# Three transformer blocks in one program: the triangular inverses of block 3 as paced steps over 128 partitions, the relative-bias rows written during block 2

## The chip, the cores and the metric

The program runs on one core of a Trainium2 chip. The metric is device time in microseconds (us) of one execution. A core has a matrix engine (TensorE, PE in the rows below, its weight loads PEld), a vector engine (VectorE, DVE), a scalar engine (ScalarE, ACT), GpSimd (POOL) and a queue engine (SyncE, SP) that issues nearly all transfers between DRAM and the core's memory. ACT can issue transfers too.

## The reference, cut to what matters

One sequence of 512 tokens with 2048 features goes through three blocks. The change concerns two pieces of block 3.

The first is the gated delta rule, in chunks of tokens. With `L` strictly lower triangular, every head and chunk needs the inverse of `I + L`:

```python
L = jnp.where(strict, jnp.einsum("bnhid,bnhjd->bnhij", k_beta, k) * decay, 0.0)
t_inv = lax.linalg.triangular_solve(eye + L, eye, left_side=True, lower=True, unit_diagonal=True)
u = jnp.einsum("bnhij,bnhje->bnhie", t_inv, v_beta)
w = jnp.einsum("bnhij,bnhjd->bnhid", t_inv, k_beta * jnp.exp(g)[..., None])
```

The second is the sliding-window attention, whose logits get a bias that depends on the distance of query and key alone:

```python
bias = rel_bias[t5_bucket(jnp.maximum(dist, 0))]          # dist = query position - key position
logits = jnp.where(valid, logits + bias, -jnp.inf)
```

Around both stand projections by large weight matrices; block 2 (spatial gating and neighbourhood attention) comes between block 1 and block 3.

## The kernel before

Activations are feature-major tiles of 128 x 512. A "unit" is one projection of 128 output columns: 16 steps over the input features, each of three products (`hi*hi`, `hi*lo`, `lo*hi`), summed in a PSUM tile `pm`. Weights come on SP's queue as 128 x 1024 chunks `wr` (three buffers). ACT copies each half of a chunk into `wh`, DVE subtracts it and leaves the rest in `wl` (five buffers each); 12 products use one half. PE's order is fixed in the program, so a late `wl` holds up PE and all that stands behind it.

`drive` runs units one after the other and, between groups of 12 products, advances up to five generators (heads of the delta rule, attention pairs). A bare `yield` of a generator means "go on 12 products later". The build then merges these streams into one fixed order per engine; each engine goes through its rows in order.

**Inverses.** `gdn` makes four generators `inverse(g)`, each for two heads. `inverse_blocks` takes the 32 x 32 diagonal blocks of both heads (32 blocks), writes them to DRAM (`du`) and reads them back with one block per partition (`fs`, 32 partitions). Then 31 steps of substitution run on DVE, step `i` being a product of `i*i` elements into `fp` and a sum into row `i` of `ft`. The result goes back over DRAM (`dt`) into the heads' tiles `acc...`/`km`. All 31 steps are issued in one go, then 16 bare yields pass before the heads may use the result. `inverse_join` (run by `scan`) transposes on DVE and joins the blocks on PE.

**Relative bias.** `rel_bias` makes 16 rows of 384 values (one small product on PE, one sum on DVE) and writes 128 copies of each to DRAM (`reld`, 3 MB) on SP's queue. The attention pairs of block 3 read it back (`t<-reld`). `block3` calls it ahead of `small_products`, which loads `w3s` in six chunks through the same `wr` buffers and the same queue.

`mods` is background work: 1024-column tiles `gr` of two more weight matrices, loaded on SP's queue and summed on DVE during blocks 1 and 2. Its tags `gr` and `ga` are those of `fs`, `fp` and `ft`.

Of the kernel before, what the change touches and what calls it, by code (L numbers as in the profile page):

```python
# [18 lines left out]
P = 128  # L19
# [9 lines left out]
INV_STEPS = 16  # L29
# [10 lines left out]
class Kernel:  # L40
# [44 lines left out]
    def t(self, tag="w", dt=F32):  # L85
        """A [128, 512] tile; each tag hands out its slots in order, so streams that overlap have their own."""
        self.n += 1
        return self.tp.tile([P, T], dt, name=f"t{self.n}", tag=tag, bufs=SLOTS[tag])
# [40 lines left out]
    def tr4(self, src):  # L129
        """128x128 transposes of the four column blocks of src into one bank."""  # L130
# [5 lines left out]
    def rsqrt_cols(self, out, ss, scale, eps):  # L136
        """out = (ss * scale + eps) ** -0.5 on [128, n] with n small."""
# [5 lines left out]
    def bcast_cols(self, cols):  # L143
        """[128, 4] token columns -> [128, 512] rows, the same on every partition (in PSUM)."""
# [23 lines left out]
    def unit_steps(self, w, ct, rhs):  # L168
        """z^T of 128 columns: w is [ct, half, 128, 1024]; rhs the (hi, lo) tiles of each k. Pauses every 12 products."""
# [16 lines left out]
    def first_units(self, w, cts, make):  # L186
        """The first units of a block, k by k, while make(k) gives the (hi, lo) tiles of their operand."""
# [28 lines left out]
    def drive(self, todo, width, fillers=(), done=None):  # L216
        """Runs generators beside the stream of units. A generator yields either a unit that it needs, whose PSUM it
        is sent, or None: products that wait for other engines then come a few products of the stream later.
        Generators start in the order of todo, up to width at a time; fillers keep the stream going beyond that.
        done holds the units that are there already."""  # L220
# [58 lines left out]
    def silu2(self, z, rows=None):  # L279
        """2 * silu of a unit's PSUM (times rows)."""  # L280
# [9 lines left out]
    def block1(self):  # L290
# [5 lines left out]
        # the operand is gain * x; the rms factor of a token is put on every unit as it leaves its PSUM  # L296
# [27 lines left out]
        # lb = (1 + th) / 2; f = lb + (1 - lb) * (1 + tanh(z / 2)) / 2  # L324
# [17 lines left out]
    def gate(self, ys, i, w, ct, h, rows=None):  # L342
        """ys[i] *= 2 * silu(unit)."""
        g = self.silu2((yield w, ct, h), rows)
        while ys[i] is None:
            yield
        self.tt(ys[i], ys[i], g)

    def hgrn(self, hd, h, w, ys):
# [31 lines left out]
        # chunk states  # L381
# [52 lines left out]
    def softmax_block(self, sc, n, bias, den, s_out):  # L434
        """sc holds -scores in PSUM; bias is -bias. Leaves exp(s - max) in s_out and its sum in den."""
# [4 lines left out]
    def pipeline(self, n, *stages):  # L440
        """Stage s of item i runs in step i + s, the later stages first."""
# [6 lines left out]
    def stack_q(self, z):  # L448
        """For each of the two 64-feature heads of z: its hi part on one half of the partitions, lo on the other."""
# [9 lines left out]
    def stack_k(self, z, new):  # L459
        """For each head of z: (hi on both halves, lo on both halves). Scores then take two passes over 128 rows."""  # L460
# [61 lines left out]
    def turn(self, pr, nb):  # L522
        """The transposes of nb 128x128 blocks."""
# [7 lines left out]
    def pv(self, pt, vt, out, vs):  # L531
        """out = P @ v from turned P; vs lists (block of vt, columns within it)."""
# [4 lines left out]
    def finish_pair(self, po, den):  # L537
        """Normalised [128 q, 4, 2, 64] -> feature-major [128, 512]."""
# [24 lines left out]
    def mods(self, wada, c, b, mod):  # L563
        """mod[128, 48] = silu(c) @ w_ada + b_ada, feature f at [f % 128, f // 128]."""
# [33 lines left out]
    def stat_end(self, lasts):  # L598
        """Token columns [128, 4] of every sum, in one PSUM tile."""
# [11 lines left out]
    def feature_mean(self, out, src):  # L611
        """Mean over one tile's 128 features, on every partition."""
# [4 lines left out]
    def out1(self, ys):  # L617
# [27 lines left out]
        # var(u) + LN_EPS * (mean(x1^2) + EPS): the layer norm of the rms-normalised rows  # L645
# [922 lines left out]
```

## Time and profile before

| What | Value |
|---|---|
| median of 3 runs (lowest to highest) | 3509.61 us (3507.68 to 3515.55) |
| profiled execution: its span | 3507.8 us |
| PE busy | 3406.7 us, 97% |
| DVE busy | 2070.1 us, 59% |
| ACT, POOL busy | 1273.5 us, 322.3 us |
| the chain that ended last | PE 86%, DVE 7%, DMA 3%, issue 3% |

The profile of the profiled execution shows its time as its span from the first to the last instruction; the time around the span is not shown apart. The span lies between the lowest and the median of the three runs. A busy share is an average over three blocks: what a change in one stage can give is read from the stretches of time of that stage.

### The profile page before, as it was taken

Reading aid. Unit: us, or ns where it says so; the run is one execution under the profiler, and the core shown is the slowest. Engines: PE = TensorE matmul, PEld = TensorE weight load, DVE = VectorE, ACT = ScalarE, POOL = GpSimd, SP = SyncE. Lnnn points to the kernel's source line nnn. Section 1 sums busy time; section 2 is a strip of 40 time slices with the busy share of each in tenths; the row PEclk is TensorE's granted clock in tenths of the full one; section 3 lists DMA queues with packets and bytes.
Section 4 is the critical chain, followed back from the end, with each engine's and each line's share of the span. In section 5 each row is a group of like instructions: output and inputs, shape, how many; then the busy total and the mean of one; then the engine's idle time right before and its main releaser. Section 6 shows DMA issues by size and latency. Waiting matters only on the chain.

```text
span 3507.8 us, 44459 instructions
## 1 busy us (share of the span) xinstructions
PE 3406.7 (97%) x16678; PEld 2844.2 (81%) x16678; DVE 2070.1 (59%) x3492; ACT 1273.5 (36%) x2439; POOL 322.3 (9%) x266
## 2 busy tenths in 40 slices
PE   8999999999998999999999879899989999999999
PEld 6777888888887888888888768787878888888887
DVE  8677556556776655544378738867765433344552
ACT  4222244445334223444442423232334443432331
POOL 3000000000340000110113101110100000000000
PEclk9999999999999999999999989999999999999999
DMA  6355345435663544422234252222222233334442
GB/s 217 120 168 168 128 156 180 151 120 183 221 215 109 193 162 162 139 86 89 89 117 146 77 132 79 78 85 78 76 63 79 90 103 105 120 103 139 146 144 91
DMA packets 156729, 447.82 MB, mean 128 GB/s; under 512 B 25649, under 2 KB 35169, under 8 KB 156513
## 3 DMA queue, kind: packets, MB, share of 16 engines
q1 hardware_dynamic: 156368, 444.53, 38.8%
q8 instruction: 131, 2.15, 0.3%
q14 instruction: 86, 0.70, 0.1%
q10 hardware_dynamic: 144, 0.44, 0.0%
HBM read 419.74 MB, written 25.17 MB: 127 GB/s over the span
## 4 chain that ended last, share of the span: by engine, by line
PE 86%; DVE 7%; DMA 3%; issue 3%; ACT 1%; POOL 1%; SPq 0%; DVEq 0%; ACTq 0%; POOLq 0%
PE pm L127 75%; PE x L127 8%; DMA gr<-in_wada_dram 2%; PE x L133 2%; PE x L526 1%; DVE fp L116 1%; DVE wl L116 1%; DMA wr<-in_w3s_dram 1%; DVE t L116 1%; DVE ft L1099 1%; DVE t L119 1%; DVE ga L119 1%; POOL s L141 0%; ACT t L113 0%; DMA t<-in_xt_dram 0%
## 5 line engine op out<-in xcount | busy, mean ns | idle before, releaser
L127 PE MATMUL pm<-a,wh 128*128 128x512 f32 x8512 | 2675.2, 395 | 15.9 <-ACT a L113 15.0
L127 PEld LDWEIGHTS pm<-a,wh 128*128 128x128 f32 x8512 | 1580.7, 189 | 333.9 <-ACT a L113 16.9
L127 PE MATMUL pm<-a,wl 128*128 128x512 f32 x4256 | 1671.4, 393 | 5.2 <-DVE wl L116 5.2
L116 DVE TENSOR_TENSOR wl<-wr,wh 128x512 fp32r<-128x512 f32 (+1 forms) x1080 | 766.1, 713 | 988.2 <-ACT wh L113 925.5
L113 ACT ACTIVATE wh<-wr 128x512 fp32r<-128x512 f32 (+1 forms) x1080 | 676.1, 628 | 1782.6 <-PE pm L127 1631.3
L127 PEld LDWEIGHTS pm<-a,wl 128*128 128x128 f32 x4256 | 803.6, 189 | 178.6 <-DVE wl L116 7.6
L119 DVE SCALAR_TENSOR_TENSOR ga<-gr,sc_c,ga 128x1024 f32<-128x1024 f32 x180 | 237.9, 1322 | 78.6 <-DMA gr<-in_wada_dram 77.6
L127 PEld LDWEIGHTS x<-t,t 128*128 128x128 f32 (+2 forms) x1552 | 195.1, 188 | 37.3 <-issue 9.4
L127 PE MATMUL x<-t,t 128*128 128x128 f32 (+4 forms) x1552 | 208.7, 277 | 8.5 <-DVE t L116 4.7
L113 ACT ACTIVATE t<-x 128x512 f32<-128x512 f32 (+3 forms) x325 | 156.0, 496 | 122.2 <-PE x L127 65.4
L141 POOL TENSOR_TENSOR s<-s,nhalf 128x4 f32<-128x4 f32 (+1 forms) x51 | 63.3, 1241 | 1285.8 <-DVE s L124 1285.8
L113 ACT ACTIVATE t<-t 128x512 f32<-128x512 f32 (+1 forms) x172 | 106.7, 629 | 136.5 <-DVE t L119 83.7
L116 DVE TENSOR_TENSOR t<-t,t 128x512 f32<-128x512 f32 (+1 forms) x195 | 137.7, 706 | 21.6 <-ACT t L113 17.8
L113 ACT ACTIVATE t<-t,s 128x128 f32<-128x128 f32 (+2 forms) x192 | 98.6, 514 | 82.6 <-DVE s L437 63.5
L116 DVE TENSOR_TENSOR fp<-ft,fs 32x1 f32<-32x1 f32 (+30 forms) x124 | 97.0, 782 | 1.8
L133 PE MATMUL x<-cst,t 128*128 128x128 f32 x496 | 75.3, 278 | 12.6 <-DVE t L116 7.2
L133 PEld LDWEIGHTS x<-cst,t 128*128 128x128 f32 x496 | 61.3, 143 | 28.6 <-issue 8.0
L596 POOL TENSOR_TENSOR acc<-acc,t 128x512 f32<-128x512 f32 x42 | 73.8, 1783 | 86.8 <-DVE t L119 72.7
L116 DVE TENSOR_TENSOR a<-t,a 128x512 fp32r<-128x512 f32 x112 | 77.5, 710 | 4.0 <-ACT a L113 3.8
L526 PE MATMUL x<-cst,t 128*128 128x128 f32 x464 | 74.5, 275 | 4.1 <-ACT t L113 4.1
L119 DVE SCALAR_TENSOR_TENSOR t<-t,pm 128x512 f32<-128x512 f32 x64 | 43.7, 683 | 46.4 <-PE pm L127 46.0
L113 ACT ACTIVATE a<-t 128x512 fp32r<-128x512 f32 x112 | 66.4, 621 | 10.4 <-DVE t L119 9.3
(215 smaller groups left out, 1812.6 us busy)
## 6 DMA issues: line engine op xcount, KB each, us to landing
wr<-in_w_dram SPq DMA_DIRECT2D x380, 512.0 KB, 3.3
gr<-in_wada_dram SPq DMA_DIRECT2D x192, 512.0 KB, 4.2
wr<-in_wo_dram SPq DMA_DIRECT2D x96, 512.0 KB, 3.4
wr<-in_w_dram SPq DMA_DIRECT2D x48, 256.0 KB, 3.1
t<-in_xt_dram SPq DMA_DIRECT2D x32, 256.0 KB, 3.8
res<-t SPq DMA_DIRECT2D x32, 256.0 KB, 2.2
t<-res SPq DMA_DIRECT2D x32, 256.0 KB, 2.7
gld<-t SPq DMA_DIRECT2D x32, 256.0 KB, 2.0
```

The lines of the kernel that those rows point to most:

```text
L113: return self.nc.scalar.activation(out, in_, fn, **kw)
L116: return self.nc.vector.tensor_tensor(out, a, b, op)
L119: return self.nc.vector.scalar_tensor_tensor(out, a, s, b, op0=op0, op1=op1)
L127: return self.nc.tensor.matmul(out, l, r, start=start, stop=stop, skip_group_check=True)
L133: self.nc.tensor.transpose(b[:, p * P:(p + 1) * P], src[:, p * P:(p + 1) * P], self.ident)
L141: self.nc.gpsimd.tensor_tensor(out, u, self.nhalf[:, :n], OP.pow)
L526: self.nc.tensor.transpose(b[:, j * P:(j + 1) * P], pr[:, j * P:(j + 1) * P], self.ident)
L596: self.nc.gpsimd.tensor_tensor(self.acc[i], self.acc[i], src, OP.add)
L1099: nc.vector.tensor_reduce(tm[:B, 32 * i:32 * i + i], pv, AX, OP.add, negate=True)
```

## The change

`INV_STEPS` goes from 16 to 5 and `INV_RUN = 3` is new. The 32 columns of each inverse are cut into four quarters of 8, and each quarter has its own 32 partitions, so that 128 partitions work. Step `i` is then a product of `8*(i+1)` elements and a sum. `fs` is loaded four times, once for each quarter. `inverse_blocks` is a generator now: a bare yield stands ahead of the steps and one after every third (10 of them), then five follow, so that the count of 16 yields stays. `fp` and `ft` have tags of their own. The result comes out transposed, so `inverse_join` starts from the transpose. `rel_bias` is called at the start of `block2`, and its write to `reld` is issued by ACT. The diff also drops comments and docstrings, which are left out here.

```diff
-INV_STEPS = 16
+INV_STEPS = 5
+INV_RUN = 3
...
     def block2(self, h, first):
         w = self.A["w2"]
         ys = [None] * 16
+        self.rel_bias()
...
-    def inverse_blocks(self, ats, f0s):
+    def inverse_blocks(self, ats, e0s):
...
-        pr = self.gp.tile([P, 1024], F32, name=f"fp{self.n}", tag="gr", bufs=2)
-        tm = self.gp.tile([P, 1024], F32, name=f"ft{self.n}", tag="ga", bufs=1)
+        pr = self.gp.tile([P, 256], F32, name=f"fp{self.n}", tag="fp", bufs=1)
+        tm = self.gp.tile([P, 256], F32, name=f"ft{self.n}", tag="ft", bufs=1)
...
-        nc.sync.dma_start(fs[:B], du)
-        nc.gpsimd.memset(tm[:B], 0.0)
-        nc.gpsimd.memset(tm[:B, ::33], 1.0)
-        fv = fs[:B].rearrange("p (j i) -> p j i", i=32)
-        tv = tm[:B].rearrange("p (i c) -> p c i", c=32)
+        for q in range(4):
+            nc.sync.dma_start(fs[B * q:B * q + B], du)
+        nc.gpsimd.memset(tm, 0.0)
+        for q in range(4):
+            nc.gpsimd.memset(tm[B * q:B * q + B, 8 * q:8 * q + 232:33], 1.0)
+
+        nc.vector.memset(fs[:, ::33], -1.0)
+        fv = fs.rearrange("p (j i) -> p j i", i=32)
+        tv = tm.rearrange("p (c j) -> p c j", j=32)
+        yield
         for i in range(1, 32):
-            pv = pr[:B, :i * i].rearrange("p (c j) -> p c j", j=i)
-            self.tt(pv, tv[:, :i, :i], fv[:, None, :i, i].to_broadcast([B, i, i]))
-            nc.vector.tensor_reduce(tm[:B, 32 * i:32 * i + i], pv, AX, OP.add, negate=True)
-        nc.sync.dma_start(dt, tm[:B])
+            m = i + 1
+            pv = pr[:, :8 * m].rearrange("p (c j) -> p c j", j=m)
+            self.tt(pv, tv[:, :, :m], fv[:, None, :m, i].to_broadcast([P, 8, m]))
+            nc.vector.tensor_reduce(tv[:, :, i], pv, AX, OP.add, negate=True)
+            if i % INV_RUN == 0:
+                yield
+        nc.sync.dma_start(dt.rearrange("b (q e) -> q b e", q=4), tm)
...
-        e = self.t()
-        nc.vector.transpose(e, f0)
+        e, f = e0, self.t()
+        nc.vector.transpose(f, e0)
...
-            self.inverse_blocks([ks[a][3] for a in heads], f0s[2 * g:2 * g + 2])
+            yield from self.inverse_blocks([ks[a][3] for a in heads], f0s[2 * g:2 * g + 2])
...
-        nc.sync.dma_start(self.reld, mk[0:16, None, 0:384].to_broadcast([16, P, 384]))
+        nc.scalar.dma_start(self.reld, mk[0:16, None, 0:384].to_broadcast([16, P, 384]))
...
     def block3(self, h, first):
-        self.rel_bias()
```

How the change moves instructions is seen at three places. First SP's queue where block 3 begins: `w3s` are the loads of `small_products`, `gld` are gates that go to DRAM. Before:

```order
674 L1384 DMA gld<-t_16750 128x512
675 L1384 DMA gld<-t_16753 128x512
676 L155 DMA wr_16913<-in_w3s_dram 128x816
677 L1384 DMA gld<-t_16756 128x512
678 L1279 DMA reld<-t_16741 2048x1x384
679 L155 DMA wr_16963<-in_w3s_dram 128x816
680 L155 DMA wr_17013<-in_w3s_dram 128x272
```

Now:

```order
674 L1394 DMA gld<-t_16750 128x512
675 L1394 DMA gld<-t_16753 128x512
676 L156 DMA wr_16913<-in_w3s_dram 128x816
677 L1394 DMA gld<-t_16756 128x512
678 L156 DMA wr_16963<-in_w3s_dram 128x816
679 L156 DMA wr_17013<-in_w3s_dram 128x272
```

The 3 MB write no longer stands ahead of the last two loads. It is issued by ACT instead, between the first units of block 2 and the next (`pm` are units' sums, `wh` the weights' first halves):

```order
706 L114 ACTIVATE t_9301<-pm_8825 128x512
707 L114 ACTIVATE t_9376<-pm_8826 128x512
708 L1290 DMA reld<-t_9259 2048x1x384
709 L114 ACTIVATE t_9417<-pm_9327 128x512
710 L114 ACTIVATE wh_512_9430<-wr_9424 128x512
711 L114 ACTIVATE wh_0_9474<-wr_9472 128x512
```

What stands behind it on ACT are a unit's activation and the weights of the units that follow.

The second place is DVE in the middle of the first inverse. Before, between two weight halves:

```order
2143 L116 TENSOR_TENSOR wl_0_18202<-wr_18199,wh_0_18201 128x512
2144 L116 TENSOR_TENSOR fp_17618<-ft_17619,fs_17617 32x625
2145 L1099 TENSOR_REDUCE ft_17619<-fp_17618 32x25
2146 L116 TENSOR_TENSOR wl_512_18206<-wr_18199,wh_512_18205 128x512
2147 L116 TENSOR_TENSOR fp_17618<-ft_17619,fs_17617 32x676
2148 L1099 TENSOR_REDUCE ft_17619<-fp_17618 32x26
2149 L116 TENSOR_TENSOR wl_0_18257<-wr_18254,wh_0_18256 128x512
```

Now, at the end of the first inverse and the start of the second, without rows between (row 2155 is the new diagonal of the second inverse's `fs`):

```order
2151 L117 TENSOR_TENSOR wl_512_18191<-wr_18184,wh_512_18190 128x512
2152 L117 TENSOR_TENSOR fp_17618<-ft_17619,fs_17617 128x248
2153 L1109 TENSOR_REDUCE ft_17619<-fp_17618 128x8
2154 L117 TENSOR_TENSOR fp_17618<-ft_17619,fs_17617 128x256
2155 L1101 MEMSET fs_17954 128x32
2156 L1109 TENSOR_REDUCE ft_17619<-fp_17618 128x8
2157 L117 TENSOR_TENSOR wl_0_18254<-wr_18251,wh_0_18253 128x512
2158 L117 TENSOR_TENSOR fp_17955<-ft_17956,fs_17954 128x16
2159 L1109 TENSOR_REDUCE ft_17956<-fp_17955 128x8
2160 L117 TENSOR_TENSOR wl_512_18258<-wr_18251,wh_512_18257 128x512
```

The products are at most 256 long instead of up to 961, and as before each weight half has its place between them. The second inverse begins one weight half behind the first one's last sum (before, seven other rows stood there).

The third place is PE where the first head joins its blocks. Before, the first product read the tile `acc` that the transfer had filled, and two weight halves (`wl`) lay between the last one that DVE makes ahead of the inverse's last sum and that product. Now it reads the transpose that DVE makes (`t_18237`), and no half lies between: `wl_512_18191`, of row 2151 above, is the last one ahead of it.

```order
8884 L128 MATMUL pm_18183<-a_16472,wl_512_18191 128x512
8885 L134 MATMUL x_18231<-cst,t_18175 128x128 x4
8886 L128 MATMUL x_18243<-t_18237,t_18239 128x128 x4
8887 L128 MATMUL pm_18183<-a_16553,wh_0_18253 128x512
8888 L128 MATMUL pm_18183<-a_16554,wh_0_18253 128x512
8889 L128 MATMUL pm_18183<-a_16553,wl_0_18254 128x512
```

On DVE that transpose has row 2180, 22 rows behind row 2158 above, with the second inverse's first steps and two more weight halves between. SP issues the result's write as one transfer, printed `4x32x256` (before `32x1024`).

## Rows read from the trace of the kernel before

**Rows 1.** The head of the page and its first part: busy time, share of the span and instructions of each engine.

```profile
span 3507.8 us, 44459 instructions
PE 3406.7 (97%) x16678; PEld 2844.2 (81%) x16678; DVE 2070.1 (59%) x3492; ACT 1273.5 (36%) x2439; POOL 322.3 (9%) x266
```

**Rows 2.** Busy time by stretch around `small_products`, where block 3 begins. Columns: stretch and its length, then for PE, PEld, DVE, ACT and POOL the busy us (instructions), the granted TensorE clock as a share of full speed, the DMA engines' busy share, GB/s.

```profile
2020.00:2040.00 20.00, 19.99 (x151) 18.71 (x149) 4.83 (x11) 4.17 (x10) 0.00 (x0) 1.00 0.90 146
2040.00:2058.00 18.00, 0.00 (x0) 0.00 (x0) 0.00 (x0) 0.23 (x1) 0.00 (x0) 0.59 0.90 142
2058.00:2064.00 6.00, 5.75 (x26) 5.75 (x27) 2.88 (x6) 2.56 (x7) 0.00 (x0) 0.53 0.58 200
```

**Rows 3.** PE's waits over the whole span: the first row, which line waited for which, us in total, times, the longest.

```profile
PE pm L127 <- ACT wh L113: 18.3, 1, 18.3
```

**Rows 4.** The timeline of SP's queue at the same place (start, us, instruction).

```profile
2022.36 0.68 SPq L1279 DMA_DIRECT2D reld<-t  x1
2024.36 8.83 SPq L155 DMA_DIRECT2D wr<-in_w3s_dram  x1
```

**Rows 5.** The chain that ended last, in order of time (start, us, what): one transfer at that place, and a group of 12 products of a unit further on.

```profile
2024.36 33.30 DMA wr<-in_w3s_dram
...
2412.74 2.73 PE pm L127 x12
```

**Rows 6.** The view of the DMA issues: what, engine, count, KB each, median us from issue to landing.

```profile
reld<-t SPq DMA_DIRECT2D x1, 3072.0 KB, 33.6
wr<-in_w3s_dram SPq DMA_DIRECT2D x5, 408.0 KB, 4.8
fs<-du SPq DMA_DIRECT2D x4, 128.0 KB, 2.2
dt<-ft SPq DMA_DIRECT2D x4, 128.0 KB, 2.1
acc<-dt SPq DMA_DIRECT2D x24, 16.0 KB, 2.6
wr<-in_w3s_dram SPq DMA_DIRECT2D x1, 136.0 KB, 24.8
```

**Rows 7.** Busy time by stretch in block 3 (columns as in rows 2): the stretches of the inverses, and those ahead of them and between them.

```profile
2100.00:2140.00 40.00, 40.00 (x208) 33.81 (x207) 27.05 (x44) 15.72 (x27) 9.50 (x10) 1.00 0.27 86
2140.00:2270.00 130.00, 117.24 (x579) 96.09 (x578) 123.29 (x216) 35.09 (x62) 18.57 (x20) 0.95 0.23 73
2270.00:2350.00 80.00, 79.27 (x412) 66.95 (x412) 45.58 (x79) 28.65 (x51) 12.56 (x13) 1.00 0.30 95
2350.00:2412.00 62.00, 56.46 (x289) 47.20 (x288) 57.44 (x100) 14.67 (x28) 5.00 (x5) 0.94 0.21 64
2412.00:2500.00 88.00, 87.28 (x454) 73.87 (x453) 50.69 (x92) 30.81 (x55) 14.01 (x15) 1.00 0.28 91
2500.00:2580.00 80.00, 71.62 (x381) 61.13 (x381) 73.99 (x129) 20.48 (x38) 11.24 (x7) 0.94 0.20 58
```

**Rows 8.** The same view of the instructions that write or read `fp` alone (DVE's busy us and count, clock, DMA share, GB/s): the products and sums of the first two inverses.

```profile
2140.00:2270.00 130.00, 78.54 (x124) 0.95 0.23 73
```

**Rows 9.** DVE's groups of instructions from 2140 to 2600 us, first over all shapes, then by shape: line, operation, out<-in, shapes, count, busy us, mean ns of one, idle time before them and what ended it.

```profile
L116 DVE TENSOR_TENSOR fp<-ft,fs 32x1 f32<-32x1 f32 (+30 forms) x124 | 97.0, 782 | 1.8
L116 DVE TENSOR_TENSOR wl<-wr,wh 128x512 fp32r<-128x512 f32 x118 | 81.2, 693 | 62.7 <-ACT wh L113 58.0 <-PE x L127 2.5 <-PE x L133 2.1
L1099 DVE TENSOR_REDUCE ft<-fp 32x1 f32<-32x1 f32 (+30 forms) x124 | 60.2, 486 | 1.8
...
L116 DVE TENSOR_TENSOR fp<-ft,fs 32x961 f32<-32x961 f32 x4 | 7.5, 1882 | 0.0
L1099 DVE TENSOR_REDUCE ft<-fp 32x31 f32<-32x961 f32 x4 | 4.5, 1134 | 0.0
...
L116 DVE TENSOR_TENSOR fp<-ft,fs 32x1 f32<-32x1 f32 x4 | 0.6, 140 | 0.0
L1099 DVE TENSOR_REDUCE ft<-fp 32x1 f32<-32x1 f32 x4 | 0.5, 135 | 0.0
```

**Rows 10.** DVE's timeline in the first inverse: two weight halves that follow each other; between them stand two products and a sum of the inverse.

```profile
2184.55 0.67 DVE L116 TENSOR_TENSOR wl<-wr,wh 128x512 fp32r<-128x512 f32 x1
...
2189.20 0.67 DVE L116 TENSOR_TENSOR wl<-wr,wh 128x512 fp32r<-128x512 f32 x1
```

**Rows 11.** Busy time by stretch where block 2 begins (columns as in rows 2).

```profile
1120.00:1180.00 60.00, 60.00 (x291) 50.10 (x290) 31.00 (x78) 15.78 (x28) 3.39 (x3) 1.00 0.32 101
1180.00:1225.00 45.00, 45.00 (x209) 37.40 (x208) 35.07 (x60) 11.99 (x20) 2.38 (x2) 1.00 0.83 282
```

**Rows 12.** What SP's queue waited for from 1060 to 1300 us, before it issued a weight load (us in total, times, the longest).

```profile
SPq L155 <- DVE wl L116: 128.4, 37, 25.7
```

**Rows 13.** SP's timeline behind the first inverse: the result's write, and the reads into the two heads' tiles.

```profile
2202.18 0.34 SPq L1100 DMA_DIRECT2D dt<-ft  x1
...
2205.28 4.56 SPq L1104 DMA_DIRECT2D acc<-dt  x8
```

**Rows 14.** The instructions that write or read `ft`: POOL's two fills of it (min/median/max ns, first and last start).

```profile
L1092 POOL MEMSET ft<- x4: 941/942/947, 1508.6 to 2412.1; 32x1024 f32 x4
L1093 POOL MEMSET ft<- x4: 145/146/149, 1509.6 to 2413.1; 32x32 f32 x4
```

More of the change, by code (lines that the diff above doesn't have):

```diff
@@ L1104, in inverse_blocks, with inverse_join @@
                 nc.sync.dma_start(
-                    f0s[a][32 * b:32 * b + 32, :].rearrange("j (n i) -> j n i", i=P)[:, :, 32 * b:32 * b + 32],
-                    dt[p0:p0 + 4].rearrange("n (j i) -> j n i", i=32))
-    def inverse_join(self, at, f0):
+                    e0s[a][32 * b:32 * b + 32, :].rearrange("c (n i) -> c n i", i=P)[:, :, 32 * b:32 * b + 32],
+                    dt[p0:p0 + 4].rearrange("n (c i) -> c n i", i=32))
+    def inverse_join(self, at, e0):
         nc = self.nc
@@ L1117, in inverse_join @@
         nc.gpsimd.tensor_tensor(v4(c2), v4(at), m(1), OP.mult)
-        f = f0
         for lv, c in ((0, c1), (1, c2)):
```

## The prediction, made before the changed kernel ran

> **What bounds the kernel now.** I read the page's busy times first: PE is busy for 97% of 3507.8 us, DVE for 59% [rows 1]. The products don't change in number, so a gain can only come out of PE's idle time and of the time in which its clock is low; both are found stretch by stretch in the view by windows. Two places belong to this change.
>
> Where block 3 begins, PE has no work from 2040 to 2058 us, and up to 2064 us it runs at a granted clock of 0.53 [rows 2]. The view of waits has this as one wait of 18.3 us, the longest of all [rows 3], for ACT's halves of a weight. The chain says what ACT waited for: a load of `w3s` under way for 33.30 us [rows 5], where the median of five such loads is 4.8 us [rows 6]. It was issued 2.0 us after the 3 MB write to `reld` [rows 4], which needs 33.6 us [rows 6]: 2022.4 + 33.6 = 2056.0, and the load lands at 2057.7. It came right behind the write in the same queue.
>
> In the three stretches of the inverses DVE is busy for 123.3 of 130, 57.4 of 62 and 74.0 of 80 us, and PE idles for 12.8, 5.5 and 8.4 us; ahead of them and between them DVE is busy for 57 to 68%, PE idles for at most 0.7 us, and the clock is 1.00 [rows 7]. Of these 254.7 us of DVE 157.2 are the inverses': 97.0 us of products and 60.2 us of sums, 39.3 us for each of the four [rows 9]; the first two inverses fill 78.5 us of the first stretch [rows 8]. They take turns with the weights, and so delay them: in the first inverse two weight halves start 4.65 us apart [rows 10], while PE uses one in 2.73 us [rows 5].
>
> **The change part by part.**
>
> *The write leaves SP's queue in block 3.* The idle 18.3 us go, and so does what the clock cost from 2058 to 2064 us, 6 x (1 - 0.53) = 2.8 us: 21 us. Below that I go only if the last loads are late for another reason: at 4.8 us a load, the one issued at 2024.4 lands at 2029, long before PE runs dry at 2040. Bounds 18 to 21 us; I take 21.
>
> *The same write in block 2.* The transfer keeps its 33.6 us, in which the engines were 0.90 busy. From 1120 to 1180 us they are 0.32 busy, from 1180 on 0.83 [rows 11]. Beside a share of 0.32 the write gets 0.68: 33.6 x 0.90 / 0.68 = 44 us, which ends at about 1165 us, just ahead of the dense stretch. Weight loads slow down meanwhile, but are not what PE waits for there: SP holds them back until DVE has freed a buffer, 37 times, 128.4 us in all [rows 12], and PE is never idle. Bounds: nothing, and 20 us if the weights stand behind the whole write (a rival below); I take 1 us. On ACT the issue takes about SP's 0.68 us [rows 4] and stands behind a sum on DVE that comes ahead of it by then; a unit's activation and weight halves wait behind it, at no cost to a PE that has halves in stock. The three small loads and PE's one product only move.
>
> The Trainium skill ("DMA: Bandwidth & Descriptors", section "Issuing engines are not separate DMA queues") says that transfers from ACT's and SP's queues share the same 16 engines and interleave, so that a second queue saves only issue time. By this rule the queue itself brings nothing, and block 2's loads would be slowed by the write rather than stand behind it, which would take most of its chance from the second rival below. No row here shows two queues under load at once, and I leave that chance as it is.
>
> *The inverses' work on DVE.* A step now has 8(i+1) elements in place of i squared: 4,216 over 31 steps instead of 10,416. The fixed part is 140 ns for a product and 135 ns for a sum, the slope (1882 - 140) / 960 = 1.81 ns and (1134 - 135) / 960 = 1.04 ns an element [rows 9]. So 31 x 0.140 + 4,216 x 1.81 ns = 12.0 us of products, 31 x 0.135 + 4,216 x 1.04 ns = 8.6 us of sums, 20.6 us in place of 39.3. The new products read one operand without gaps; at the slope of the weights' subtraction, (693 - 140) / 512 = 1.08 ns, they would take 8.9 us, 17.5 us in all. I take 19.5 us: 20 us saved for each inverse, 80 us in all. DVE's share falls to (123.3 - 40) / 111 = 75% in the first stretch, 37 / 53 = 71% in the second, 54 / 67 = 81% in the third (each stretch shortened by what PE loses in it). Ahead of them 68% left PE without idle time [rows 7], so most of its loss should go, not all.
>
> What there is to win: 26.7 us idle, and by the clock at most 130 x 0.05 + 62 x 0.06 + 80 x 0.06 = 15.0 us (part of the low clock lies in the idle time and costs nothing), 41.7 us. I keep 6 us of it for a DVE that is still at 71 to 81%.
>
> *New waits.* `fs` is loaded four times, 2.2 us each and overlapped, and DVE's diagonal waits for it; the first sits four rows later in DVE's order than the first product did, so I cost it at nothing (0 to 2 us if that cover is gone). POOL's fills of `ft`: one of 128 x 256 and four small ones at 0.145 us; against 0.94 us for 32 x 1024 [rows 14] between 0.24 and 0.94, so about 1.0 us with the small ones. Only where the second inverse follows the first does DVE stand: its first product waits for this fill, the fill for the landing of `dt`, which waits for the last sum. With 2.1 us as before [rows 6]: 0.3 + 2.1 + 1.0, less one weight half of 0.7, is 2.7 us of an idle DVE. Behind it come two weight halves and three steps of a convolution of about their length, 5 x 0.7, and nine products and eight sums of 16 to 80 elements, 17 x 0.2, some 7 us, and then the transpose for which PE's first join product waits. From the last sum on that is 10 to 11 us; the tile it reads is there by then, since half of the 4.56 us of issues [rows 13] and a landing of 2.6 us [rows 6] behind `dt` make 0.3 + 2.1 + 2.3 + 2.6 = 7.3 us. PE has up to four halves in stock (five buffers), 4 x 2.73 = 11 us. So it waits for 0 to 2 us with a fast landing.
>
> But the write's outermost dimension is now four. If only 4 of the 16 DMA engines (the number over which the profile takes its DMA share) carry it, 128 rows of 1 KB are 32 to an engine; the `reld` write has 2048 rows of 1.5 KB, 128 to an engine, in 33.6 us, 0.26 us a row, so that `dt` lands after up to 8.4 us instead of 2.1, and PE waits for up to 8 us and then starts at the low clock (some 3 us more). Bounds 0 to 11; I take 6. The other joins come a head or more later, with cover.
>
> The Trainium skill speaks against this part of the change ("DMA: Bandwidth & Descriptors", section "Why a DMA increments its semaphore by 16 and not by 1"): the number of engines is the largest divisor, up to 16, of the outermost dimension of both sides, so a dimension of four gives four engines. By that the term stands nearer to 11 than to 0. No `dt` of such a shape is in the trace; whether it holds shows in its landing.
>
> *The start of the program.* The first inverse's `ft` has a tag of its own, so its fills move from 1508 us [rows 14] to the start: 1 us of POOL, beside a PE that is not waiting for POOL there. I cost it at nothing (-2 to +2).
>
> **Sum.** 3507.8 - 21 + 1 - (41.7 - 6 - 6) = 3458.1 us against the profiled span. That span lies 1.8 us below the runs' median, so against the median 3460 us.
>
> **Rivals.**
>
> *The readback takes the place of the bursts.* For: the four-fold cut, DVE's handover with no other work in it, PE's product right behind the last half. Against: only the first join is without cover. Price: 11 us instead of 6 at the join, and some 6 us for weights that come late after the handover: 3471 us.
>
> *Block 2's weights stand behind the write, as `w3s` did.* For: in block 3 a load behind the write took 33.30 us. Against: it is another queue, and loads run ahead. With three chunks of 24 products in stock, 3 x 5.5 = 16 us, PE would idle for 33.6 - 16 = 17 us and lose 3 us to the clock: block 2 gives back what block 3 gains, 3480 us.
>
> *Slower: every `dt` lands very late.* Each inverse's result passes this one write, and PE's order has no other work at the join. PE would lose landing + 8 - 10 us, with the clock a fifth more. With a landing of 20 us at all four: 4 x 1.2 x 18 = 86 us of loss, less the 6 counted: 3540 us. It decides from about 14 us (4 x 1.2 x 12 = 58). For it speaks a load of 136 KB that took 24.8 us behind another transfer [rows 6]; against it, that nothing large is in the queues there (DMA share 0.20 to 0.30 [rows 7]).
>
> *The change doesn't do what it says* can't be for the amount of work on DVE; for the pacing it can: between two weight halves the order has as few of the inverse's rows as before. I count on the shorter rows alone.
>
> **How the numbers follow.** The forecast, 3460 us, has 0.70; the readback 0.15; the write in block 2 0.09; the slower case 0.06, a third of it close to no change. The range begins where all is won and the start gains 2 us, 3509.6 - 21 - 42 - 2 = 3444.6, and reaches past the two nearer rivals, which can meet with smaller parts, to 3484: 3443 to 3484. Runs of this kernel tell some 0.2%, 7 us, from no change; faster by more than that 0.94, within it 0.02, slower 0.04.
>
> **What would show it.** In the profile after: `w3s` loads of about 5 us and no idle stretch of PE at the start of block 3; a `reld` write of 34 to 60 us from ACT in block 2 with PE busy throughout; 8 to 12 us of products and about 8.6 us of sums for each inverse, DVE at 70 to 80% where it was 92 to 95%, and PE's idle time there down from 26.7 us to under 10; the landing of `dt`, 2 or 8 us. I am wrong if PE idles in block 2 under the write, if the products take more than 12 us, or if PE's waits at the first join come to more than 11 us.

## The result and the profile after

| | before | after |
|---|---|---|
| median (lowest to highest), 4 runs each | 3511.66 us (3507.68 to 3515.55) | 3488.89 us (3486.6 to 3494.16) |
| ratio, 95% interval | | 0.9935 [0.992, 0.995] |
| profiled execution: its span | 3507.8 us | 3484.9 us |

The changed kernel is faster by 22.8 us; 50 were forecast, and 3488.9 lies outside the range of 3443 to 3484 us. The direction was right, the size was not. The head of its page, which answers to [rows 1]:

```profile
span 3484.9 us, 44515 instructions
PE 3400.8 (98%) x16678; PEld 2841.0 (82%) x16678; DVE 2008.9 (58%) x3496; ACT 1273.6 (37%) x2439; POOL 322.9 (9%) x278
```

DVE lost 61 us of work, where 80 were forecast. In the rows below `...` stands for rows of the same view that are left out. Busy time by stretch (columns as in [rows 2]): block 2's start, which answers to [rows 11]; the start of block 3, which now begins 18 us later, so that the stretch of the old 18.3 us wait [rows 2, 3] is 2058 to 2076; and the inverses, which answer to [rows 7]:

```profile
1120.00:1180.00 60.00, 48.42 (x220) 39.12 (x219) 24.79 (x66) 12.02 (x22) 3.02 (x3) 0.91 0.68 130
...
2058.00:2076.00 18.00, 17.25 (x96) 14.82 (x95) 12.17 (x50) 6.95 (x21) 0.00 (x0) 1.00 0.43 144
...
2140.00:2200.00 60.00, 51.80 (x244) 43.15 (x244) 51.08 (x133) 15.85 (x27) 8.60 (x13) 0.91 0.29 86
...
2350.00:2400.00 50.00, 46.64 (x250) 38.26 (x248) 39.54 (x95) 12.83 (x24) 6.44 (x10) 1.00 0.28 85
...
2500.00:2580.00 80.00, 74.97 (x415) 63.19 (x414) 56.37 (x116) 23.45 (x45) 8.24 (x6) 1.00 0.22 70
```

Block 3's start is full. Block 2, where PE was busy for 60.00 of 60 us, now has 11.6 us of idle time and a granted clock of 0.91. The inverses still lose 8.2, 3.4 and 5.0 us, and the clock is low in the first stretch only.

**Block 2.** PE's longest wait from 1100 to 1200 us, then ACT's timeline:

```profile
PE x L134 <- ACT t L114: 9.8, 1, 9.8
```

```profile
1127.83 0.66 ACTq L1290 DMA_DIRECT2D reld<-t  x1
1140.08 0.60 ACT L114 ACTIVATE t<-pm 128x512 f32<-128x512 f32 x1 [12.01 <-PE pm L128]
1140.57 2.70 ACT L114 ACTIVATE wh<-wr 128x512 fp32r<-128x512 f32 x5
1162.83 1.15 ACT L114 ACTIVATE wh<-wr 128x512 fp32r<-128x512 f32 x2 [19.55 <-DMA wr<-in_w_dram]
```

Behind the write ACT stands for 12.01 us at an activation that needs a unit PE is still at work on; five weight halves stand behind that activation. It is row 709 of ACT's order in the part on the change. Before, four halves came ahead of that activation:

```order
707 L113 ACTIVATE t_9366<-pm_8826 128x512
708 L113 ACTIVATE wh_512_9420<-wr_9414 128x512
709 L113 ACTIVATE wh_0_9464<-wr_9462 128x512
710 L113 ACTIVATE wh_512_9468<-wr_9462 128x512
711 L113 ACTIVATE wh_0_9504<-wr_9502 128x512
712 L113 ACTIVATE t_9407<-pm_9317 128x512
```

So no buffer comes free, and behind its row at 1125.98 SP issues no weight load until 1146.09. The chain that ended last then shows what the next load met, the second that SP issued there:

```profile
1125.98 0.42 SPq L681 DMA_DIRECT2D t<-in_b_sp_dram  x1
1146.09 22.10 SPq L156 DMA_DIRECT2D wr<-in_w_dram  x5
```

```profile
1147.30 18.08 DMA wr<-in_w_dram
```

A load that takes 3.3 us as a median took 18.08 under the write. It lands at 1165.4; PE had run dry.

**The first join.** DVE, SP, POOL and PE where the first inverse ends, which answers to [rows 13]:

```profile
2183.18 0.18 DVE L117 TENSOR_TENSOR fp<-ft,fs 128x16 f32<-128x16 f32 x1 [4.14 <-POOL ft L1099]
...
2184.09 1.28 DVE L117 TENSOR_TENSOR fp<-ft,fs 128x24 f32<-128x24 f32 x1
...
2185.62 1.02 DVE L117 TENSOR_TENSOR fp<-ft,fs 128x32 f32<-128x32 f32 x1
...
2191.86 0.70 DVE L1126 STREAM_TRANSPOSE t<-acc 128x512 f32<-128x512 f32 x1
...
2192.60 0.67 DVE L120 SCALAR_TENSOR_TENSOR t<-t,t 128x512 f32<-128x512 f32 x1
...
2178.47 0.66 SPq L1112 DMA_DIRECT2D dt<-ft  x1
...
2182.68 0.31 POOL L1097 MEMSET ft<- 128x256 f32 x1 [16.95 <-DMA dt<-ft]
...
2183.69 1.63 POOL L1128 TENSOR_TENSOR t<-t,cst 128x512 f32<-128x512 f32 x1
2185.28 1.29 POOL L1129 TENSOR_TENSOR t<-t,cst 128x512 f32<-128x512 f32 x1
...
2193.42 1.09 PE L134 MATMUL x<-cst,t 128*128 128x128 f32 x4 [6.42 <-DVE t L120]
```

The result's write has landed by 4.2 us after its issue (2178.47 to 2182.68, when POOL may fill), DVE idles for 4.14 us, and PE for 6.42. Behind this wait the clock is low for a while:

```profile
2180.00:2200.00 20.00, 13.58 (x60) 11.38 (x60) 14.97 (x40) 4.11 (x7) 3.61 (x7) 0.83 0.30 92
```

**DVE's cost of a step**, which answers to [rows 9]: the two groups of the four inverses.

```profile
L117 DVE TENSOR_TENSOR fp<-ft,fs 128x16 f32<-128x16 f32 (+30 forms) x124 | 54.3, 438 | 6.6 <-POOL ft L1099 4.1
...
L1109 DVE TENSOR_REDUCE ft<-fp 128x8 f32<-128x16 f32 (+30 forms) x124 | 36.4, 293 | 2.5
```

### The profile page after: what moved, and what is told of

It reads as the page before. It is cut to its first block, busy times and chain, and to the rows that moved or that the text cites. A ratio compares the mean times of both kernels' runs of the same rounds, so it can differ in the third digit from the quotient of the medians.

```text
span 3484.9 us, 44515 instructions
## 1 busy us (share of the span) xinstructions
PE 3400.8 (98%) x16678; PEld 2841.0 (82%) x16678; DVE 2008.9 (58%) x3496; ACT 1273.6 (37%) x2439; POOL 322.9 (9%) x278
## 4 chain that ended last, share of the span: by engine, by line
PE 87%; DVE 6%; issue 3%; DMA 3%; POOL 1%; ACT 1%; SPq 0%; DVEq 0%; ACTq 0%; POOLq 0%
PE pm L128 75%; PE x L128 8%; DMA gr<-in_wada_dram 2%; PE x L134 2%; PE x L527 1%; DVE wl L117 1%; DVE t L117 1%; DVE ga L120 1%; DVE fp L117 1%; DMA wr<-in_w_dram 1%; DVE t L120 1%; DVE ft L1109 0%; POOL s L142 0%; DMA t<-in_xt_dram 0%; ACT t L114 0%
## 5 line engine op out<-in xcount | busy, mean ns | idle before, releaser
L128 PEld LDWEIGHTS x<-t,t 128*128 128x128 f32 (+2 forms) x1488 | 187.9, 188 | 31.9 <-issue 9.4
L128 PE MATMUL x<-t,t 128*128 128x64 f32 (+3 forms) x1488 | 200.6, 277 | 5.2 <-DVE t L117 4.9
L748 POOL TENSOR_TENSOR t<-cst,t 128x256 f32<-128x256 f32 x48 | 41.2, 891 | 351.7 <-DMA t<-in_rpb_dram 274.2
L114 ACT ACTIVATE t<-pm 128x512 f32<-128x512 f32 (+2 forms) x154 | 68.6, 482 | 13.5 <-PE pm L128 13.3
```

Of the source, the lines that this page charges most:

```text
L114: return self.nc.scalar.activation(out, in_, fn, **kw)
L128: return self.nc.tensor.matmul(out, l, r, start=start, stop=stop, skip_group_check=True)
L748: nc.gpsimd.tensor_tensor(rows(nbs[hh][cb]), self.mask_na[:, None, v * 32:v * 32 + 32].to_broadcast([P, 8, 32]), sv[:, :, off:off + 32], O ...
```

## The experiments

Executions of one kernel differ by 3 to 13 us, more than several of the terms. The ratios are to executions of the kernel before that were taken beside each run; their median lay between 3508.8 and 3513.7 us, so that medians of different rows compare to some us only. So next to the medians stand three marks of each profiled execution: the start of the first load of `wo` (end of block 1), of `w3s` (end of block 2) and of `wbg` (end of block 3's heads). What lies between two marks is compared. A row from which such a mark is read, of the kernel before, profiled once more:

```profile
L155 SPq DMA_DIRECT2D wr<-in_wo_dram x96: 327/328/825, 849.6 to 3479.1; - x96
```

| Kernel | median us | ratio to before, 95% | `wo` | `wo` to `w3s` | `w3s` to `wbg` |
|---|---|---|---|---|---|
| before (the execution shown) | | | 845.2 | 1162.9 | 1122.7 |
| before, once more | 3513.4 (one execution) | | 849.6 | 1161.7 | 1123.3 |
| after | 3488.9 | 0.9935 [0.992, 0.995] | 849.3 | 1176.8 | 1081.4 |
| rel_only | 3505.8 | 0.9984 [0.9975, 0.9994] | 849.5 | 1176.4 | 1102.3 |
| inv_only | 3495.8 | 0.9951 [0.9937, 0.9966] | 852.1 | 1162.7 | 1102.9 |
| rel_pool2 | 3487.5 | 0.9923 [0.9906, 0.9939] | 855.1 | 1174.6 | 1081.5 |
| rel_sp2 | 3487.2 | 0.9924 [0.9907, 0.9941] | 849.0 | 1174.7 | 1081.3 |
| rel_bg | 3477.1 | 0.9898 [0.9877, 0.9918] | 851.4 | 1164.4 | 1083.3 |
| rel_bg_act1 | 3487.1 | 0.9936 [0.9918, 0.9953] | 854.8 | 1178.3 | 1081.7 |
| inv_dt16 | 3487.2 | 0.9932 [0.9918, 0.9947] | 853.4 | 1177.6 | 1077.3 |
| inv_ft2 | 3489.0 | 0.9937 [0.9922, 0.9952] | 851.8 | 1178.1 | 1079.5 |
| comb3 | 3468.8 | 0.9884 [0.9868, 0.9901] | 848.8 | 1162.1 | 1077.5 |
| comb4_12 | 3470.0 | 0.9889 [0.9872, 0.9906] | 851.2 | 1163.5 | 1077.5 |
| comb4_20 | 3472.2 | 0.9891 [0.9877, 0.9906] | 855.5 | 1162.9 | 1078.6 |

**The halves of the change.** inv_only calls `rel_bias` in block 3 again, with SP's queue; rel_only has the old inverses and the new `rel_bias`.

> The change of the inverses alone: rel_bias is called in block 3 again and its write issued by SP, as before. By the traces of before and after (block 3 as a whole won 41 us, of which the write's removal 21; the start lost 4): 20 won by the inverses less 4 at the start, so 3511.7 - 16 = about 3495 us, with the 18 us wait for w3s still there. By the prediction's own terms (29.7 won, start 0): 3482 us.

> The change of the relative bias alone: the inverses are those of before, rel_bias is called in block 2 and its write issued by ACT. By the traces: 21 won where block 3 begins, 15 lost in block 2: 3511.7 - 6 = about 3506 us, with PE idle for about 12 us between 1140 and 1170 us. By the prediction's own terms (21 won, 1 lost): about 3492 us. If the 4 us at the start belong to the inverses' new tile, they are not here; if they belong to the moved rel_bias, they are.

The first row is inv_only's, PE's longest wait; the second rel_only's, block 2:

```profile
PE pm L128 <- ACT wh L114: 18.2, 1, 18.2
```

```profile
1100.00:1200.00 100.00, 89.17 (x408) 73.15 (x407) 50.56 (x109) 32.56 (x54) 3.02 (x3) 0.95 0.57 129
```

Both came out as the traces had it. Of the medians the parts are 17.9 and 7.9 us, 25.8 together, where the whole change won 22.8; the spread of the executions covers the difference. By the marks, against the mean of the two profiles of before (1162.3 and 1123.0), the inverses win 20.1 us, the write's leave from block 3 wins 20.7, and its arrival in block 2 costs 14.1 (rel_only) or 14.5 (after).

**The kernel before, once more.**

> The kernel before, unchanged, profiled once more. The profiled execution shown of it began its last loads of block 1 (wo) at 845.2 us, the changed kernel at 849.3 us. If this is what the change does to the start, this run shows 845 again; if executions differ by as much, it shows some 849 us, and a span of about 3512 us.

The mark stands at 849.6 us, the span is 3511.6. So executions differ there by as much as the first comparison showed, and the one shown of before was a quick one. That does not make the start free of the change. PE's waits up to 110 us have a row in the changed kernel that neither execution of before has, nor rel_only with its old inverses:

```profile
PE x L128 <- DVE acc L407: 1.5, 1, 1.5
```

All eleven kernels with the new inverses have it, with 1.1 to 2.7 us, and begin `wo` at 848.8 to 855.5 us; the three executions with the old ones begin it at 845.2, 849.6 and 849.5. Why the new inverses bring this wait is open.

**Which engine issues the write.** The same write in the same place, from POOL and from SP:

```diff
-        nc.scalar.dma_start(self.reld, ...)
+        nc.gpsimd.dma_start(self.reld, ...)     # rel_pool2
+        nc.sync.dma_start(self.reld, ...)       # rel_sp2
```

> The changed kernel with one edit: the 3 MB write to reld stands at the same place of block 2 but is issued by POOL. ACT's order there is then again as before the change (four weight halves ahead of the activation that waits for PE), while the transfer is the same one at the same time. Theory 1 (ACT's order): the loss in block 2 comes from the activation that now stands ahead of five weight halves on ACT, so that no weight load is issued for 20 us. Then PE waits at most 2 us between 1100 and 1200 us, and the time is 3488.9 - 15 = about 3474 us. Theory 2 (the engines): the loads stand behind the write because both use the same 16 DMA engines, whatever queue issues them. Then PE still idles for 10 us or more there and the time is about 3489 us.

> The changed kernel with one edit: the write to reld at the same place of block 2, but issued by SP, in the queue of the weight loads. ACT's order is as before the change. Theory 1 (ACT's order alone makes the loss): about 3474 us, PE waits at most 2 us between 1100 and 1200 us. Theory 2 (the loads stand behind the write in any queue): a load issued behind it takes about 33 us, as w3s did before, PE idles for 10 to 20 us and the time is 3489 to 3495 us. If only sharing a queue puts loads behind the write, this run is slow (3489 to 3495) while the run with POOL's queue is not.

rel_pool2: two stretches, the write (with the us from issue to landing), a load out of the chain that ended last, and ACT's next halves:

```profile
1127.00:1180.00 53.00, 52.08 (x232) 41.73 (x231) 15.51 (x32) 13.81 (x25) 2.26 (x2) 1.00 0.80 152
...
1225.00:1250.00 25.00, 19.37 (x89) 15.59 (x90) 23.20 (x54) 3.10 (x6) 2.38 (x2) 0.86 0.61 196
```

```profile
reld<-t POOLq DMA_DIRECT2D x1, 3072.0 KB, 35.1
```

```profile
1144.42 23.45 DMA wr<-in_w_dram
```

```profile
1161.04 1.15 ACT L114 ACTIVATE wh<-wr 128x512 fp32r<-128x512 f32 x2 [11.94 <-DMA wr<-in_w_dram]
```

Both theories were half right. A load took 23.45 us beside the write here, so another queue does not spare it; but with ACT's halves in their old order the stock was full, and PE lost 0.9 of 53 us. Instead 5.6 us of idle time and a low clock came at 1225 us, long after the write: in DVE's order the second group of layer-norm statistics, whose square roots POOL makes, now stands behind 368 weight halves of the program instead of 341. In rel_sp2 three small loads stood behind the write in the same queue. They were issued from 1129.6 to 1142.0 us and landed 32.9, 28.7 and 24.9 us later (3 to 5 us in the changed kernel), and PE waited for the second of them:

```profile
PE x L128 <- DMA t<-in_sgu_b_dram: 5.9, 1, 5.9
```

Block 2 is longer by 12.3 and 12.4 us. From ACT and from POOL, what the issuing engine handles next has moved back in the program's order. That the build takes the engine as busy for the whole transfer is an inference; for it speaks that a write of 16 rows at the same place (built, not run) leaves the four halves ahead of the activation. From SP it is the queue: the three small loads follow the same five weight loads in the order as in the changed kernel, and there only the write came between.

**The write elsewhere, in pieces or whole.** rel_bg makes the bias as a third background task behind `mods`, in the tile that `mods` leaves free:

```diff
+        self.bgq.append(self.rel_bias())
...
+        for j in range(0, P, 8):
+            nc.sync.dma_start(self.reld[:, j:j + 8], mk[:, None, :].to_broadcast([16, 8, 384]))
+            yield
```

rel_bg_act1 has the same place, but one write of 3 MB from ACT.

> The changed kernel, but the relative bias is made behind the background sums of blocks 1 and 2: its tile is the one that mods uses, its write is cut into 16 pieces of 192 KB, one for each weight load, issued by SP from about 1440 us on, where the DMA engines are 0.27 busy. Theory 1 (what costs in block 2 is the order around one 3 MB write: rows of the issuing engine, and what they feed, are put behind it): without such a block nothing is put off, PE idles for less than 2 us more than before in block 2, and the time is 3488.9 - 15 = about 3474 us. Theory 2 (3 MB through the engines costs some 15 us wherever it stands): about 3489 us.

> The relative bias behind the background sums, but as one write of 3 MB issued by ACT, as in the changed kernel, some 300 us later. Behind it on ACT stand six copies and activations of 64 to 256 columns that wait for PE, then the next weight half. Theory 1 (one large write puts rows of its issuing engine behind, and SP's loads then run beside it): weight loads of 10 to 20 us and PE idle for 8 to 12 us at about 1530 to 1570 us, 3485 to 3489 us. Rival (only the place at the start of the block was bad, the engines are 0.27 busy here): PE idles for less than 3 us, 3476 to 3480 us.

rel_bg, block 2's start, the stretch of the 16 pieces, and the pieces:

```profile
1120.00:1180.00 60.00, 60.00 (x284) 49.85 (x283) 28.62 (x73) 18.33 (x30) 3.40 (x3) 1.00 0.36 118
...
1520.00:1620.00 100.00, 100.00 (x511) 84.02 (x510) 40.42 (x82) 46.26 (x112) 10.19 (x12) 1.00 0.42 117
```

```profile
reld<-relg SPq DMA_DIRECT2D x16, 192.0 KB, 3.7
```

rel_bg_act1, where the write was issued at 1537.1 us: ACT behind it, and the stretch in which PE stands:

```profile
1547.36 1.21 ACT L114 ACTIVATE t<-pm 128x256 f32<-128x256 f32 x4 [7.71 <-PE pm L128]
...
1568.63 0.63 ACT L114 ACTIVATE wh<-wr 128x512 fp32r<-128x512 f32 x1 [13.98 <-DMA wr<-in_w_dram]
```

```profile
1560.00:1570.00 10.00, 0.20 (x1) 0.20 (x2) 0.71 (x2) 1.11 (x2) 0.00 (x0) 0.53 0.96 222
```

In pieces, issued from 1534.0 to 1612.9 us (later than expected), the write costs PE nothing while it runs, and block 2 is longer by 2.1 us. Whole, at that same quiet place, it costs 16.0, about what it costs at the block's start. So the place is not the cause; that the 3 MB go in one write is. The two runs differ in the issuing engine too, which made little difference at the block's start. And ACT again stood behind a row that waits for PE (7.71 us) before it stood for a load (13.98), so that the two effects of the single write are not told apart here either. Pieces at the block's start were not run.

**The handover of the inverses.** inv_dt16 writes each result in four transfers of 32 rows; inv_ft2 gives `ft` two buffers (and `fp` the tile of `mods`, for room).

```diff
-        nc.sync.dma_start(dt.rearrange("b (q e) -> q b e", q=4), tm)
+        for q in range(4):
+            nc.sync.dma_start(dt[:, 256 * q:256 * q + 256], tm[B * q:B * q + B])
```

> The changed kernel, but each inverse's result is written by four transfers of 32 rows each instead of one whose outermost dimension is four. Theory 1 (the shape is why the result lands late): the fill of the second inverse's tile starts about 2 us after the last of the issues instead of 4.2, DVE's idle time of 4.1 us at the handover falls to 2 to 3 us (three more issues of about 0.4 us), and PE's wait of 6.4 us at the first join to 4 to 5 us: 3488.9 - 2 = about 3487 us. Rival (the shape costs nothing, 4.2 us is what such a write takes): the four issues come on top, the idle time grows to 5 us and the time is 3489 to 3491 us.

> The changed kernel, but ft has two buffers (fp has moved into the tile of mods, for room), so that the second inverse waits for no landing. Theory 1 (the handover makes PE's wait at the first join): DVE's idle time of 4.1 us there is gone, PE's wait of 6.4 us falls to about 2 us and its clock stays up: 3488.9 - 7 = about 3482 us. Rival (DVE's rows that stand ahead of the join's operands make the wait, not the idle time): PE waits for 5 us or more, and the time is 3487 to 3489 us.

inv_dt16: the landing of a piece, DVE's idle time, PE's wait. Behind them inv_ft2's wait:

```profile
dt<-ft SPq DMA_DIRECT2D x16, 32.0 KB, 1.5
```

```profile
2186.89 0.18 DVE L117 TENSOR_TENSOR fp<-ft,fs 128x16 f32<-128x16 f32 x1 [2.01 <-POOL ft L1099]
```

```profile
PE x L134 <- DVE ft L1109: 3.1, 1, 3.1
```

```profile
2195.75 1.09 PE L134 MATMUL x<-cst,t 128*128 128x128 f32 x4 [6.21 <-DVE t L120]
```

In pieces of 32 rows a piece lands in 1.5 us, and POOL may fill 3.0 us after the first of the four issues (2183.38 to 2186.39) in place of 4.2. DVE's idle time and PE's wait are halved, and the stretch `w3s` to `wbg` is 4.1 us shorter; in the medians that is lost in their spread (3487.2 against 3488.9). With two buffers DVE never idles, yet PE waits for 6.21 us as before: DVE now goes on with the second inverse, whose products up to 120 elements stand ahead of the convolution that PE waits for. The rival was right there: what DVE does ahead of that operand makes the wait, idle or not. (From `w3s` to `wbg` the run is 1.9 us shorter than the change, which the median does not show.)

**Together.** comb3 has rel_bg's and inv_dt16's edits. comb4_12 and comb4_20 also start the second inverse 12 or 20 bare yields later.

> The relative bias behind the background sums, in 16 pieces, together with the inverses' results written by four transfers of 32 rows. Each alone won 11.8 and 1.7 us against the changed kernel. If they add up: 3477 - 2 to 4 = 3473 to 3475 us. If the four transfers win nothing: 3477 us.

> As the run before, and the second inverse starts 12 bare yields later, so that 5 instead of 7 of its steps stand on DVE ahead of the transpose that the first join needs. Theory (DVE's rows ahead of the join's operands, not the idle time, make PE's wait there): 2 steps of 0.5 us and a little, PE's wait at the first join falls by 1 to 2 us: 3472 to 3474 us. Rival (the wait is for the transfers behind dt): as without the shift.

> The same with 20 bare yields: no step of the second inverse stands ahead of that transpose, 2 of the next ones do in the later pairs, where now transposes stand among the steps. By the theory that DVE's rows make the wait: PE's wait of 3 to 8 us at the first join falls to 0 to 2 us, 3468 to 3472 us, unless the second inverse is now late for heads 2 and 3, which shows as a new wait there (3475 or more).

comb3 takes 3468.8 us, 20 less than the change under study (18.6 by the marks, 17 to 18 by the ratios), and beats both kernels; 3473 to 3477 were expected. The later start is of no further use that shows: 3470.0 (3467.2 to 3477.8) and 3472.2 us (3468.0 to 3476.0). With 12 yields PE waits for 3.2 us at the join, without them (comb3) for 3.0. With 20 that is 1.6 us, yet from `w3s` to `wbg` the program takes 1078.6 us where comb3 takes 1077.5: PE waits for DVE's convolution later on (5.7 us in place of 0.7).

## Why the prediction was wrong

**The write out of block 3: right.** 21 us forecast, 20.7 measured. The last loads of `w3s` take 3.3 us, and PE is busy for 17.25 of 18 us where it stood still.

**The write in block 2: the step that failed.** +1 us was forecast, +14.5 came, near the rival's 20, which had a chance of 0.09. What failed is the overlap: the write was to stretch to 44 us beside the loads, and the loads to slow down at no cost. The write did not stretch: issued by ACT it took 34.1 us (rel_only), 34.9 (inv_dt16) and 34.5 (rel_bg_act1), and it was the loads that gave way, from 3.3 us to 18.08 in the changed kernel and 23.45 in rel_pool2. Two sentences were wrong. "Weight loads slow down meanwhile, but are not what PE waits for there" holds only as long as the stock is full. And behind the issue on ACT "a unit's activation and weight halves wait [...] at no cost": the order in the part on the change had shown that activation ahead of the halves, and it needs a PE that comes to it 12 us later. The two meet: without the halves no load is issued for 20 us, and the loads that follow need 18 us beside the write. In rel_pool2, with the stock full, slow loads cost 0.9 us while they last. No run has the moved order without the large transfer, so the share of each is open. The rival's own picture was right for one queue and not for two. On SP's queue the first small load behind the write landed at 1129.6 + 32.9 = 1162.5 us, 33.7 us after the write's issue at 1128.8, about as long as the write takes. On another queue a load issued after the write landed ahead of it (rel_pool2: halves at 1161.0, the write's end at 1134.9 + 35.1 = 1170).

On the rule of the Trainium skill ("DMA: Bandwidth & Descriptors", section "Issuing engines are not separate DMA queues") the runs agree twice: from ACT, POOL and SP the write costs block 2 the same 12 to 15 us, so that a second queue brings no time; and loads from SP beside a write from POOL are slowed, up to 23.45 us, but the first of them is not held to the write's end. What the prediction made of it, that slowed loads lower the rival's case, does not follow.

**The inverses: right in kind, 9.6 us too high.** 29.7 forecast, 20.1 measured (inv_only). Where 12 us were to stay (6 at the join, 6 elsewhere), 21.3 did: at the first stretch 8.2 idle and 51.8 x 0.09 = 4.7 by the clock, then 3.4 and 5.0. Three terms were mis-sized.
- The work: products 54.3 / 4 = 13.6 us for each inverse (10.9 taken between 12.0 and 8.9), sums 9.1 (8.6). The longest product, 632 ns, has a slope of (632 - 170) / 240 = 1.93 ns an element: the operand without gaps makes it no cheaper, and the lower end had no ground. 22.7 us each, 16.6 saved in place of 20. How much of PE's loss comes from this is not told apart.
- The join: 6.4 idle and, behind it, 13.58 x 0.17 = 2.3 by the clock are 8.7; 6 was taken, of at most 11. What PE waits for is the convolution's last row on DVE (2192.60), which PE's order has ahead of the join product, and not the transpose that the prediction named. The landing (4.2) was between the two ends, but two small products took 1.0 to 1.3 us where some 0.2 were counted. Over the 110 us from 2140 on DVE is busy for 87.0, 79% where 75% was forecast for 111 us.
- Elsewhere: 12.6 us where 6 were kept. PE waits there for operands of the scan and the convolution, not for weights. That the bursts cost PE through late weights was the wrong picture: in the kernel before, too, PE's waits in these stretches are nearly all for `t` and `S`, none for a `wl`. The rival with the readback had 6 us for late weights; behind the handover none came late. The two largest groups of waits of before, from 2100 to 2660 us:

```profile
PE x L127 <- DVE S L119: 10.3, 4, 3.8
PE x L127 <- ACT t L113: 8.3, 5, 3.3
```

That four engines carry the `dt` write, by the section "Why a DMA increments its semaphore by 16 and not by 1" of the same page of the Trainium skill, agrees in its direction: with an outermost dimension of 32 the same 128 KB landed in 2.1 us in one write [rows 6], and within 3.0 us of the first issue in four; with a dimension of four it took 4.2. How many engines carried it no view shows. The estimate of 8.4 us from the `reld` rows was too high.

**Pacing: right, and stronger than said.** "I count on the shorter rows alone": with the yields between the steps taken out and 15 put behind them, the build gives the same rows in the same order on all five engines, so such a kernel is this one. The word "paced" describes the source, not the program.

**The start: not settled.** 0 us was forecast, within 2. The 4 us that the first comparison showed are within what executions of the kernel before differ by; but the wait of 1.1 to 2.7 us for `acc` comes with the new inverses alone, and the prediction did not have it.

**The base.** The sum stood on a span of 3507.8 us, one of the fastest executions of before; the second was 3511.6. Forecast to measured: +13.5 for block 2, +9.6 for the inverses, some 4 up to the first mark (the base, with whatever the start costs), 27 of the 29 us. Of the three signs of being wrong that the prediction named, two came: PE idles in block 2 under the write, and the products take 13.6 us, more than 12. PE's wait at the first join stayed under 11.

## What to carry to other kernels

Here a large background write was cheap when it was cut into pieces that fit between two loads, on the queue that has the loads, and put where little else needs the bandwidth; in one piece it cost 12 to 16 us, whichever queue issued it. When an issue moves to another engine, read the order behind it for the first row that waits for someone else: all that stands behind that row comes after that wait. And a stage's gain is worked out from what PE waited for in that stage by name, not from DVE's busy share.

## What the runs showed of the hardware

A small DVE product of 0.2 to 0.3 us takes 1.0 to 1.3 us when it starts beside one of POOL's two tile products of 1.3 to 1.6 us: 128x24 and 128x32 in after (above). In inv_ft2, whose order has other products there, it is those that meet POOL's at 2187.65 and 2188.89:

```profile
2188.05 1.06 DVE L117 TENSOR_TENSOR fp<-ft,fs 128x88 f32<-128x88 f32 x1
...
2189.43 1.00 DVE L117 TENSOR_TENSOR fp<-ft,fs 128x96 f32<-128x96 f32 x1
...
2187.65 1.29 POOL L1128 TENSOR_TENSOR t<-t,cst 128x512 f32<-128x512 f32 x1
2188.89 1.36 POOL L1129 TENSOR_TENSOR t<-t,cst 128x512 f32<-128x512 f32 x1
```

Without such a neighbour 128x88 took 0.29 us in after and 0.32 in inv_dt16, and each of the four slow ones ends within 0.2 us behind one of POOL's products. The Trainium skill ("SBUF — State Buffer", section "SBUF: two separate sides") has it that the two engines share one pair of ports as an exclusive lock, where a DVE operation with two inputs from SBUF meets a POOL operation that reads SBUF; the trace agrees. And 3 MB from 16 rows move at 3072 KB / 35.1 us = 90 GB/s (rel_pool2's write). In rel_sp2 the DMA engines show a share of 0.88 at 100 GB/s in all beside such a write (1150 to 1160 us): it fills them at a rate that weight loads in a dense stretch pass threefold (0.83 at 282 GB/s [rows 11]).
